# Input projection of a hybrid encoder layer: TensorE's instruction order written out

## The chip, the cores and the metric

The kernel runs on one core of a Trainium2 chip. The core has TensorE (PE, matrix products; its weight loads are shown as PEld), VectorE (DVE), ScalarE (ACT), GpSimd (POOL) and SyncE (SP, which here issues the DMA transfers). The metric is the device time of one execution in microseconds (us); lower is better. Each engine has its own list of instructions, and semaphores make it wait for the others.

## The reference

One layer of a bidirectional encoder, float32, 1024 tokens of width 1024. The part at issue is the mixer: one projection whose columns go to windowed attention and to a gated delta rule.

```python
h = _rms_norm(x, g_mix_pre[l])
proj = h @ w_in[l]
aq, ak, av, dqkv, dgate, dalpha, dbeta = jnp.split(proj, IN_SPLITS, axis=-1)
aq, ak = _rope(aq, positions), _rope(ak, positions)
attn_o = _window_attention(aq, ak, av, attn_sink[l])      # blocks of 128, +-128 tokens
dn_o = _gated_deltanet(dqkv, dgate, dalpha, dbeta, ...)   # conv, l2norm, chunked delta rule, 2 directions
mix = jnp.concatenate([attn_o, dn_o], axis=-1) @ w_out[l]
x = x + _rms_norm(mix, g_mix_post[l])
...
c = _memory_cross_attention(...); f = _swiglu(...)
```

In the delta rule each chunk of tokens needs a triangular solve with the matrix of products k.k, decayed; the kernel forms its inverse from blocks of 32 (the "base inverse") and combines them in two levels (to 64, then to 128).

## The kernel before

The large products are kept close to float32 by splitting: an operand is cast to a high part (`whi`, `hhi`) and the rest is kept as a low part (`wlo`, `hlo`); `split` (lines 102 and 103) does it, the cast on ACT and the subtraction on DVE or POOL. A dense product of the projection is then three matmuls (high by high, low by high, high by low).

The **projection stage** takes 22 tiles of 128 columns of `w_in`. For one tile, `load_w` fetches 512 KB, splits it, and `gemm_b` (line 259) runs 2 halves of 512 tokens x 8 steps of the contraction x 3 matmuls = 48 matmuls of 128x512 into PSUM tile `pg`. Twelve tiles are keys, queries and values of the four delta-rule heads (`D0` to `D3`); four are gates (`G`), five the attention's queries and keys (`A`), one its values (`V`). Behind each tile comes elementwise work: for the delta rule a five-tap convolution (`conv`: ACT copies, four DVE operations at line 284, a silu at 285); for the attention the rotary turn (737 to 743).

A small extra product (`wab`, line 313) gives decay and beta; lines 315 to 388 turn it into `G`, `beta`, `EG` and the sine tables.

The **small products** are float32 matmuls of 128x128 that depend on a tile just finished. `prep` (from line 440) does for each head, in two halves (`part`), the decay products `gm` (459 POOL, 460 PE, `E` on ACT 462), transposes of keys (452) with their squares (ACT 469), k.k to `U` (486, 489), k.q to `pc` and `pm` (493, 496), and transposes of queries and values. `base_inverse` (510) runs for each pair of heads 60 small DVE operations (536, 538) on the stored `U`. `levels` (548) combines blocks: transposes of `Ul` (586), masks `L5` and `L6` (587, 588), products 595 and 601, and stores `Z` to `d_pz`. `window` (624) is one block of the attention: scores `psw` (646) of four heads, a masked maximum on DVE (648), exponentials and scalings on ACT (655, 663), transposes `ptw` (669), a split, weighted sums `pow` (674), and the store of `ao` to `d_mix`. `next_windows` issues two windows, each a generator in two parts, with the second part of the window before in between.

The order in which these are issued is in strings, one letter for a function and digits for its head or tile (lines 36 to 38):

```python
ORDER_1 = "D0 P0 D1 P1 D2 P2 D3 P3 B0 B1".split()
ORDER_2 = "L0 L1 G0 G1 A4 V A0 A1 L2 L3 W W W A2 A3 G2 G3 W".split()
ORDER_3 = ("M " + "s01 W K " * 5 + "s01 K " * 3 + "s01 V V").split()
```

The strings do not settle the order on PE: a scheduler places the instructions of each engine when the program is built, by its own estimates of when inputs are ready, so that dense products of later tiles can stand ahead of small products issued earlier. Stores of `pm` are held in the list `unsaved` and issued by `save` at chosen places.

Then follows the **scan stage** (`ORDER_3`): `s` is a step of the delta rule's recurrence (products `psc`, line 790) on `kv` and `pz` loaded from `d_kv` and `d_pz` (798, 799), `W` the windows that remain, `K` and `V` keys and values of the memory tokens (921, 937). The buffers for these loads lie where the normalised input of the projection was. Output projection, cross-attention and the feed-forward part come after and are not touched.

Of the kernel before, what the change touches and what calls it, by code (L numbers as in the profile page):

```python
# [35 lines left out]
ORDER_1 = "D0 P0 D1 P1 D2 P2 D3 P3 B0 B1".split()  # L36
ORDER_2 = "L0 L1 G0 G1 A4 V A0 A1 L2 L3 W W W A2 A3 G2 G3 W".split()
# [38 lines left out]
def tile_hybrid_block(  # L76
# [176 lines left out]

    def gemm_b(whi, wlo, act, psums, nk=KT):

        for ah, p_ in zip(act, psums):
            for k in range(nk):
                for i, (w, a) in enumerate(((whi, 0), (whi, 1), (wlo, 0))):
                    nc.tensor.matmul(p_, w[:, k, :], ah[a][:, k, :], start=(k == 0 and i == 0),  # L259
                                     stop=(k == nk - 1 and i == 2))  # L260

    def proj(src_cols, eng=None):
        whi, wlo = load_w(src_cols, KT, P, eng)
        pp = [pg.tile([P, 512], F32, tag="pg", name="pg") for _ in range(2)]
        gemm_b(whi, wlo, hT, pp)
        return pp

# [6 lines left out]
    def conv(pp, ci):  # L274
# [3 lines left out]
        acc = tcv.tile([P, S], F32, tag="acc", name="acc", bufs=5)  # L278
        taps = [cols[:, t * 12 + ci:t * 12 + ci + 1] for t in range(5)]
        for hf in range(2):  # L280
            nc.scalar.copy(cp[:, 2 + hf * HALF:2 + (hf + 1) * HALF], pp[hf])
            nc.scalar.activation(acc[:, hf * HALF:(hf + 1) * HALF], pp[hf], AF.Identity, scale=taps[2])  # L282
        for t in (0, 1, 3, 4):
            nc.vector.scalar_tensor_tensor(acc, cp[:, t:t + S], taps[t], acc, ALU.mult, ALU.add)  # L284
        nc.scalar.activation(acc, acc, AF.Silu)
        return acc
# [5 lines left out]
    ws = [load_w(dcols(i, 0), KT, P, after=xload[t]) for i, t in ((1, 1), (0, 3))]  # L292
# [5 lines left out]
    kqv0 = [conv(pps[0], 4), conv(pps[1], 0)]  # L298
# [5 lines left out]
    wabr = t1.tile([P, KT, P], F32R, tag="wabr", name="wabr", bufs=1)  # L304
# [3 lines left out]
    abT = t1.tile([32, S], F32, tag="abT", name="abT", bufs=1)  # L308
    for hf in range(2):
        pp = pg.tile([P, 512], F32, tag="pg", name="pg")  # L310
        for k in range(KT):
            for a in range(2):
                nc.tensor.matmul(pp, wabr[:, k, :], hT[hf][a][:, k, :], start=(k == 0 and a == 0),
                                 stop=(k == KT - 1 and a == 1))
        nc.scalar.copy(abT[:, hf * HALF:(hf + 1) * HALF], pp[0:32, :])
    pt = small()
    for c in range(NT):
        nc.tensor.transpose(pt[:, c * 32:(c + 1) * 32], abT[:, c * P:(c + 1) * P], ident[0:32, 0:32])
    ptv = pt[:, 0:256].rearrange("p (c n) -> p c n", c=NT)
    ab = t1.tile([P, NT, 16], F32, tag="ab", name="ab")  # L320
    nc.scalar.copy(ab, ptv[:, :, 16:32])
    nc.vector.tensor_tensor(ab, ab, ptv[:, :, 0:16], ALU.add)
    dump("ab", ab)

    def s64(n):
        return t1.tile([P, NT, 8], F32, tag=n, name=n)

    xa, za, ua, ea, la = s64("xa"), s64("za"), s64("ua"), s64("ea"), s64("la")
    nc.vector.tensor_tensor(xa, ab[:, :, 0:8], bc(prm[:, 8:16], 1, (P, NT, 8)), ALU.add)
    nc.vector.tensor_scalar(za, xa, -1.0, None, ALU.mult)  # L330
    nc.vector.tensor_tensor(za, za, xa, ALU.min)
    nc.scalar.activation(za, za, AF.Exp)
    nc.vector.tensor_scalar(ua, za, 1.0, None, ALU.add)
    nc.scalar.activation(la, ua, AF.Ln)

    nc.vector.scalar_tensor_tensor(ea, ua, -1.0, za, ALU.add, ALU.subtract)
    nc.vector.reciprocal(ua, ua)
    nc.vector.tensor_tensor(ea, ea, ua, ALU.mult)
    nc.vector.tensor_tensor(la, la, ea, ALU.subtract)
    nc.vector.scalar_tensor_tensor(la, xa, 0.0, la, ALU.max, ALU.add)  # L340
# [3 lines left out]
    nc.vector.tensor_tensor(G.rearrange("p d h c -> p c (d h)"), la, bc(nega, 1, (P, NT, 8)), ALU.mult)  # L344
    nc.scalar.activation(xa, ab[:, :, 8:16], AF.Exp, scale=-1.0)
    nc.vector.tensor_scalar(xa, xa, 1.0, None, ALU.add)
    nc.vector.reciprocal(za, xa)
    nc.vector.tensor_copy(beta.rearrange("p d h c -> p c (d h)"), za)
    dump("G", G)
    dump("beta", beta)  # L350


    pt = small()
    pv = pt[:, 0:192].rearrange("p (s d n) -> p s d n", s=3, d=2)
    for d in range(2):
        gd = G[:, d].rearrange("p h c -> p (h c)")
        for i, m in enumerate((("mUi", "mL", "ones"), ("mLi", "mU", "ones"))[d]):
            nc.tensor.matmul(pv[:, i, d, :], cm[m], gd, start=True, stop=True)
    EG = sm.tile([P, 3, 2, 4, NT], F32, name="EG")
    pv = pt[:, 0:192].rearrange("p (s d h c) -> p s d h c", s=3, d=2, h=4)  # L360
    nc.scalar.activation(EG[:, :, 0], pv[:, :, 0], AF.Exp)
    for c in range(NT):
        nc.scalar.activation(EG[:, :, 1, :, c], pv[:, :, 1, :, NT - 1 - c], AF.Exp)


    MAGIC = 12582912.0
    c1 = 6.28125
    c2 = float(np.float32(np.round((2 * math.pi - c1) * 2.0 ** 21) / 2.0 ** 21))
    c3 = float(np.float32(2 * math.pi - c1 - c2))
    sinT = rt.tile([P, S], F32, name="sinT")  # L370
    cosT = rt.tile([P, S], F32, name="cosT")
    for hf in range(2):
        sl = slice(hf * HALF, (hf + 1) * HALF)
        posi = t1.tile([P, HALF], I32, tag="posi", name="posi", bufs=1)
        nc.sync.dma_start(posi, positions[0, sl].partition_broadcast(P))
        ang = t1.tile([P, HALF], F32, tag="ang", name="ang", bufs=1)
        nc.vector.tensor_copy(ang, posi)
        nc.vector.tensor_scalar(ang, ang, rope_f, None, ALU.mult)
        rn = t1.tile([P, HALF], F32, tag="rn", name="rn", bufs=1)
        nc.vector.tensor_scalar(rn, ang, 1.0 / (2.0 * math.pi), MAGIC, ALU.mult, ALU.add)  # L380
        nc.vector.tensor_scalar(rn, rn, MAGIC, None, ALU.subtract)
        for cc in (c1, c2, c3):
            nc.vector.scalar_tensor_tensor(ang, rn, -cc, ang, ALU.mult, ALU.add)
        nc.vector.tensor_scalar(ang, ang, math.pi, -math.pi, ALU.min, ALU.max)
        nc.scalar.activation(sinT[:, sl], ang, AF.Sin, scale=rope_s)
        nc.scalar.activation(cosT[:, sl], ang, AF.Sin, scale=0.5)
        nc.vector.tensor_tensor(cosT[:, sl], cosT[:, sl], cosT[:, sl], ALU.mult)
        nc.vector.tensor_scalar(cosT[:, sl], cosT[:, sl], -2.0, 1.0, ALU.mult, ALU.add)
    dump("rope", (sinT, cosT))

    pa1.close()
    pa0.close()
# [8 lines left out]
    nEG = sm.tile([P, 2, 4, NT], F32, name="nEG")  # L401
    nc.vector.tensor_scalar(nEG, EG[:, 0], -1.0, None, ALU.mult)
# [13 lines left out]
    unsaved = []  # L416

    def save(after=None):

        while unsaved:  # L420
            with ExitStack() as order_:
                if after:
                    order_.enter_context(tc.issue_after(after.ins))
                nc.sync.dma_start(*unsaved.pop(0))

    def beta_rows(g):
# [8 lines left out]
        nc.tensor.transpose(pt[0:32, 0:P], bp.rearrange("p d h c -> p (d h c)"), ident)  # L435
# [4 lines left out]
    def prep(h, kc, qc, vc):  # L440

        g, hh = h // 2, h % 2
        for src, i in ((kc, 2), (qc, 3)):
            nc.sync.dma_start(d_kv[g][:, :, hh, i].rearrange("c p n -> p c n"), src.rearrange("p (c n) -> p c n", c=NT))
        def part(b):
            c4 = slice(4 * b, 4 * b + 4)

            def turned(src):
                p_ = small()
                for j in range(4):  # L450
                    o = (4 * b + j) * P
                    nc.tensor.transpose(p_[:, j * P:(j + 1) * P], src[:, o:o + P], ident)
                return p_.rearrange("p (c n) -> p c n", c=4)


            pa = small()
            for d, (mi, ml) in enumerate((("mUi", mL_s), ("mLi", mU_s))):
                gm = t2.tile([P, 4, P], F32, tag="gm", name="gm")
                nc.gpsimd.tensor_tensor(gm, bc(G[:, d, h, c4], 2, (P, 4, P)), bc(cm[mi], 1, (P, 4, P)), ALU.mult)
                nc.tensor.matmul(pa, ml, gm.rearrange("p c n -> p (c n)"), start=(d == 0), stop=(d == 1))  # L460
            E = t2.tile([P, 4, P], F32, tag="E", name="E")
            nc.scalar.activation(E, pa.rearrange("p (c n) -> p c n", c=4), AF.Exp)

            def squares(pk, rev):
                ss = t2.tile([P, 4], F32, tag="ss4", name="ss4", bufs=4)
                for j in range(4):
                    jk = t2.tile([P, P], F32, tag="jk", name="jk")
                    o = 3 - j if rev else j
                    nc.scalar.activation(jk, pk[:, j, :], AF.Square, accum_out=ss[:, o:o + 1])
                return ss  # L470

# [7 lines left out]
            if hh and b:  # L479
                beta_rows(g)  # L480
# [24 lines left out]
            if h < 3:  # L505
                save()
# [3 lines left out]
    def base_inverse(g):  # L510
# [7 lines left out]
        if g:  # L518
            save(load)
# [1005 lines left out]
```

## Time and profile before

| | |
|---|---|
| three runs | 1581.2, 1585.76, 1586.17 us (median 1585.76) |
| profiled execution | 1581.95 us, its span 1580.1 us, mean clock of PE 0.985 |
| first dense product of the projection | at 24.0 us |
| last dense product of the projection | at 393.95 us |
| first product of the scan | at 405.64 us |
| first product of the output projection (`pmg`) | about 596 us |
| PE busy | 1503.9 us, 95% |

A row of the timeline gives the start in us, the length in us, the engine, the line of the kernel, the operation, output tile <- input tiles, shapes and how many records the row joins; in brackets the idle time before it and what ended it. Matmuls are pipelined, so the time that one takes is read from start to start of the next. A float32 product counts as two records, a transpose as one. Rows of the groups give the count, then the total busy time in us and the mean in ns, then the idle time of the engine just before and its releasers. PE's clock is the share that the chip granted, 1.00 being full.

### The profile page before, as it was taken

The page shows a single profiled execution, that of the slowest core. Times are in us where ns is not written, and L with a number is a line of the kernel's source. Part 1 is how long each engine was busy: PE and PEld are TensorE (multiplying, and loading weights), DVE is VectorE, ACT ScalarE, POOL GpSimd, SP SyncE. Part 2 cuts the span into 40 slices and gives each one's busy share as a digit, 9 for nine tenths or more (in the row PEclk, how much of TensorE's full clock was granted, in tenths as well). Part 3 has the DMA queues.
Part 4 walks back from the last instruction along what each step waited for, and adds up shares of the span by engine and source line. Part 5 has one row for each costly group of instructions (what it writes and reads, how often), then busy time and mean ns, then how long its engine had stood idle before and what let it go on. Part 6 is the DMA issues. An engine that isn't in the chain of part 4 may idle for free.

```text
span 1580.1 us, 21010 instructions
## 1 busy us (share of the span) xinstructions
PE 1503.9 (95%) x7451; PEld 1256.4 (80%) x7451; DVE 1047.9 (66%) x1609; ACT 748.8 (47%) x1504; POOL 462.1 (29%) x432
## 2 busy tenths in 40 slices
PE   6999898999899989999999999999999999999998
PEld 5777777778799867788888777788888888888786
DVE  6855977965688865444346448777768654586665
ACT  6564452246866764564335566332232332444532
POOL 2364433232234500253301140433434433100021
PEclk9999999999999999999999999999999999999999
DMA  6244337473998585454222264443335333853354
GB/s 208 67 129 120 107 107 180 134 187 111 318 293 276 164 271 184 157 187 147 74 73 94 67 206 139 125 150 121 127 110 164 100 101 106 294 202 112 107 171 162
DMA packets 260485, 242.95 MB, mean 154 GB/s; under 512 B 33672, under 2 KB 199453, under 8 KB 260381
## 3 DMA queue, kind: packets, MB, share of 16 engines
q1 hardware_dynamic: 260381, 241.62, 48.6%
q8 instruction: 58, 0.95, 0.2%
q14 instruction: 46, 0.38, 0.1%
HBM read 172.07 MB, written 66.88 MB: 151 GB/s over the span
## 4 chain that ended last, share of the span: by engine, by line
PE 74%; DVE 11%; DMA 6%; ACT 4%; issue 2%; SPq 1%; POOL 1%; DVEq 0%; POOLq 0%; ACTq 0%
PE pmg L1021 10%; PE pD L1196 7%; PE pE L1196 7%; PE pg L259 7%; PE pA L1196 6%; PE pcq L259 6%; PE pdX L1386 5%; PE pdA L1386 4%; PE pB L1196 4%; PE psc L790 3%; DVE acc L284 3%; PE pdD L1386 2%; PE pcs L1102 1%; PE pco L1128 1%; PE pck L921 1%
## 5 line engine op out<-in xcount | busy, mean ns | idle before, releaser
L102 ACT CAST whi<-wraw 128x1024 fp32r<-128x1024 f32 x108 | 113.1, 1049 | 149.7 <-DMA wraw<-in_w_gate_up_dram 30.9
L103 POOL TENSOR_TENSOR wlo<-wraw,whi 128x1024 fp32r<-128x1024 f32 x48 | 117.9, 2456 | 191.1 <-ACT whi L102 168.6
L259 PE MATMUL pg<-hhi,whi 128*128 128x512 f32 x352 | 141.0, 401 | 0.0
L259 PE MATMUL pg<-hhi,wlo 128*128 128x512 f32 x352 | 140.8, 400 | 0.0
L259 PE MATMUL pg<-hlo,whi 128*128 128x512 f32 x352 | 140.3, 399 | 0.0
L103 DVE TENSOR_TENSOR wlo<-wraw,whi 128x1024 fp32r<-128x1024 f32 x60 | 74.4, 1243 | 76.8 <-ACT whi L102 72.6
L1021 PE MATMUL pmg<-whi,b 128*128 128x512 f32 x384 | 118.4, 395 | 2.7 <-ACT whi L102 2.2
L1196 PE MATMUL pA<-s,whi 128*128 128x512 f32 x352 | 109.6, 392 | 1.4 <-ACT m L1213 1.4
L284 DVE SCALAR_TENSOR_TENSOR acc<-cp,cols,acc 128x1024 f32<-128x1024 f32 x48 | 77.2, 1610 | 19.2 <-ACT acc L282 14.0
L1021 PEld LDWEIGHTS pmg<-whi,b 128*128 128x128 f32 x384 | 71.2, 188 | 17.9 <-ACT whi L102 2.7
L259 PEld LDWEIGHTS pg<-hhi,whi 128*128 128x128 f32 x352 | 67.2, 191 | 14.4 <-issue 0.7
L259 PEld LDWEIGHTS pg<-hlo,whi 128*128 128x128 f32 x352 | 67.1, 191 | 14.2 <-issue 1.0
L259 PEld LDWEIGHTS pg<-hhi,wlo 128*128 128x128 f32 x352 | 67.4, 191 | 13.6 <-issue 0.5
L1386 PE MATMUL pdX<-dhl,whi 128*128 128x512 f32 x264 | 76.1, 390 | 1.5 <-DVE zv L1441 0.8
L1196 PEld LDWEIGHTS pA<-s,whi 128*128 128x128 f32 x352 | 65.3, 188 | 15.2 <-ACT m L1213 2.0
L1273 POOL TENSOR_TENSOR act<-act,up 128x512 f32<-128x512 f32 x33 | 50.1, 1519 | 88.0 <-DVE up L1272 53.2
L1021 PE MATMUL pmg<-wlo,b 128*128 128x512 f32 x192 | 71.4, 392 | 0.0
L1196 PE MATMUL pA<-s,wlo 128*128 128x512 f32 x176 | 68.7, 391 | 1.1 <-DVE wlo L103 1.1
L102 ACT CAST whi<-araw 128x1024 fp32r<-128x1024 f32 (+1 forms) x36 | 35.4, 982 | 71.5 <-PE pdX L1386 27.6
L1416 POOL TENSOR_SCALAR frs<-sq 128x1 f32<-128x1 f32 x8 | 11.9, 1497 | 195.5 <-ACT jk L1405 194.6
L1245 POOL TENSOR_TENSOR sr<-wraw 128x512 f32<-128x512 f32 x22 | 29.9, 1359 | 128.5 <-DMA wraw<-in_w_gate_up_dram 128.4
L103 DVE TENSOR_TENSOR wlo<-araw,whi 128x1024 fp32r<-128x1024 f32 (+1 forms) x36 | 40.8, 1133 | 39.5 <-ACT whi L102 39.4
(408 smaller groups left out, 4158.9 us busy)
## 6 DMA issues: line engine op xcount, KB each, us to landing
wraw<-in_w_gate_up_dram SPq DMA_DIRECT2D x52, 512.0 KB, 3.9
kv<-d_kv SPq DMA_DIRECT2D x32, 512.0 KB, 7.3
wraw<-in_w_in_dram SPq DMA_DIRECT2D x22, 512.0 KB, 4.7
b<-in_w_down_dram SPq DMA_DIRECT2D x20, 512.0 KB, 6.8
araw<-d_as SPq DMA_DIRECT2D x20, 512.0 KB, 3.7
pz<-d_pz SPq DMA_DIRECT2D x32, 256.0 KB, 7.1
wraw<-in_w_ckv_dram SPq DMA_DIRECT2D x16, 512.0 KB, 7.6
wraw<-in_w_out_dram SPq DMA_DIRECT2D x16, 512.0 KB, 4.1
```

Of the source, the lines that this page charges most:

```text
L102: nc.scalar.copy(hi, src)
L103: (eng or nc.vector).tensor_tensor(lo, src, f32(hi), ALU.subtract)
L259: nc.tensor.matmul(p_, w[:, k, :], ah[a][:, k, :], start=(k == 0 and i == 0), stop=(k == nk - 1 and i == 2))
L284: nc.vector.scalar_tensor_tensor(acc, cp[:, t:t + S], taps[t], acc, ALU.mult, ALU.add)
L790: nc.tensor.matmul(out[:, d, h, :], lt[:, d, h, :], rt[:, d, h, :], start=True, stop=True)
L921: nc.tensor.matmul(pp, w[:, k, :], mT[a][:, k, :], start=(k == 0 and i == 0), stop=(k == KT - 1 and i == 2))
L1021: nc.tensor.matmul(pp[t], act[a][:, k, tt], w_[:, kk, :], start=(k == 0 and i == 0), stop=(k == KT - 1 and i == 2))
L1102: nc.tensor.matmul(pp[:, t2_, :], q[a][:, ct, tt], kr_[b_][:, ct, :], start=(j == 0 and i == 0), stop=(j == 1 and i == 2))
L1196: nc.tensor.matmul(out_, w[a][:, k, :], xx[b_][:, k, :], start=(start and k == 0 and i == 0), stop=(k == HK - 1 and i == 2), skip_group_ch ...
L1245: nc.gpsimd.tensor_tensor(s[0], b_[:, 0:HK], b_[:, HK:], ALU.add)
L1273: nc.gpsimd.tensor_tensor(o_, o_, up, ALU.mult)
L1386: nc.tensor.matmul(banks[t], a[:, k - k0, tt], w, start=(first and k == 0 and i == 0), stop=(k == NB - 1 and i == 2), skip_group_check=not ...
```

## The change

The order of PE's instructions in the projection stage is written out and kept.

- A list `TILES` names the 22 weight tiles in order; the first two are now the keys of heads 0 and 1 (before, key and query of head 0). They are still left to the scheduler.
- After them every matmul and transpose of the stage goes through `mm` and `turn`, which tell the builder to keep PE's instructions in program order.
- The dense products are issued step by step (a step or position is three matmuls, 0 to 31 being the first two tiles; the last is 352). `PLAN` gives the position at which each piece of `prep` is issued: K transposes and squares of keys, E decay, U k.k, C k.q, Q and S transposes of queries and values, B beta rows. `LEVELS` starts the pieces of `levels` at 232, 2.4 positions apart; `WINDOWS` starts those of the first windows at 300, 0.72 apart; `WINDOWS_AHEAD` = 4 counts the pairs of windows in the stage. The decay work runs at positions 35, 51 and 58.
- A tile's results are taken off `half` by `half`; there are 6 buffers of `acc` instead of 5, 4 of `E` instead of 2.
- The key and value rows of `d_kv` are stored separately (`kt`, `vt`) instead of together (`kv`): eight more stores with runs of half the length. The list `unsaved` is gone: `pm` is stored at once. `Ul` is loaded earlier, for both halves of a head.
- In a window, the weighted sum of a block comes one block after its transposes.

The counts of products and of elementwise operations stay. ACT's table loads go from 27 to 23.

```diff
-ORDER_1 = "D0 P0 D1 P1 D2 P2 D3 P3 B0 B1".split()
-ORDER_2 = "L0 L1 G0 G1 A4 V A0 A1 L2 L3 W W W A2 A3 G2 G3 W".split()
+TILES = "k0 k1 q0 v0 q1 v1 k2 k3 q2 v2 q3 v3 G0 G1 A4 V A0 A1 A2 A3 G2 G3".split()
+PLAN = {
+    "K0": (36, 39), "K1": (44, 47), "E0": (50, 52), "E1": (54, 56), "U0": (59, 61), "U1": (66, 68), "B0": (71,),
+    "C0": (74, 76), "Q0": (79, 82), "S0": (87, 90), "C1": (99, 101), "Q1": (104, 107), "S1": (115, 118),
+    "E2": (109, 111), "E3": (113, 121), "K2": (131, 133), "U2": (136, 138), "K3": (147, 149), "U3": (152, 154),
+    "B1": (157,), "C2": (163, 165), "Q2": (168, 171), "S2": (179, 182), "C3": (195, 197), "Q3": (200, 203),
+    "S3": (211, 214),
+}
+LEVELS = (232, 2.4)
+WINDOWS = (300, 0.72)
+WINDOWS_AHEAD = 4
...
+    def mm(*a, **k):
+        t = nc.tensor.matmul(*a, **k)
+        if pinned[0]:
+            tc.keep_in_program_order(t)
...
-    ws = [load_w(dcols(i, 0), KT, P, after=xload[t]) for i, t in ((1, 1), (0, 3))]
+    ws = [load_w(dcols(1, h), KT, P, after=xload[t]) for h, t in ((0, 1), (1, 3))]
...
-            kv = t2.tile([P, 4, 2, P], F32, tag="kv", name="kv")
...
-                        unsaved.append((d_pz[g][d][c4, :, hh, 0].rearrange("c p n -> p c n"), pm))
...
+        elif what == "K":
+            pk = turned(kqv["k", h], cs)
+            kt = t2.tile([P, 4, P], F32, tag="kt", name="kt")
+            nc.scalar.copy(kt, pk)
+            nc.sync.dma_start(d_kv[g][c4, :, hh, 0].rearrange("c p n -> p c n"), kt)
+            ss = squares(pk, False)
...
+        def weighted(j, halves):
+            for i, pe_ in enumerate(halves):
+                mm(po.rearrange("p h t -> p (h t)"), vhl[:, k0 + j, g].rearrange("p r e -> p (r e)"), pe_,
+                   start=(j == 0 and i == 0), stop=(j == nb - 1 and i == 1))
...
+    jobs, now, count = [], [32], iter(range(10000))
+    def at(pos, fn):
+        jobs.append((pos, next(count), fn))
...
+    for pos in (35, 51, 58):
+        at(pos, lambda: next(dec))
+    for what, steps in PLAN.items():
+        k, h = what[0], int(what[1])
+        for b, pos in enumerate(steps):
+            at(pos, (lambda h=h: beta_rows(h)) if k == "B" else (lambda k=k, h=h, b=b: prep(k, h, b)))
...
+    at(215, to_levels)
+    lp = level_pieces()
+    for i in range(41):
+        at(LEVELS[0] + (i - 3 if i else -6) * LEVELS[1], lambda: next(lp))
...
+    for i in range(20 * WINDOWS_AHEAD):
+        at(WINDOWS[0] + i * WINDOWS[1], window_piece)
...
+    for tok in TILES[2:]:
+        src, eng, half = weight_tile(tok[0], int(tok[1:] or 0))
+        whi, wlo = load_w(src, KT, P, eng)
+        for hf in range(2):
+            p_ = pg.tile([P, 512], F32, tag="pg", name="pg")
+            for k in range(KT):
+                for i, (w, a) in enumerate(((whi, 0), (whi, 1), (wlo, 0))):
+                    mm(p_, w[:, k, :], hT[hf][a][:, k, :], start=(k == 0 and i == 0), stop=(k == KT - 1 and i == 2))
+                if k == KT - 1:
+                    half(hf, p_)
+                now[0] += 1
+                due(now[0])
+    due(1e9)
+    pinned[0] = False
```

`to_levels` issues both base inverses and opens the pools of the levels and windows; `due` runs the jobs whose position has come; `weight_tile` gives a tile's columns and what is done with each of its halves.

More of the change, by code (lines that the diff above doesn't have):

```diff
@@ L260, in gemm_b @@
                                      stop=(k == nk - 1 and i == 2))
[L262 to L266, printed above, removed]
     pa1.close()
@@ L312, in tile_hybrid_block @@
             for a in range(2):
[L313 to L314 removed]
+                mm(pp, wabr[:, k, :], hT[hf][a][:, k, :], start=(k == 0 and a == 0), stop=(k == KT - 1 and a == 1))
         nc.scalar.copy(abT[:, hf * HALF:(hf + 1) * HALF], pp[0:32, :])
[L316 to L318 removed]
@@ L366, in tile_hybrid_block @@
[L366 to L369, printed above, removed]
+    EG = sm.tile([P, 3, 2, 4, NT], F32, name="EG")
+    nEG = sm.tile([P, 2, 4, NT], F32, name="nEG")
     sinT = rt.tile([P, S], F32, name="sinT")
     cosT = rt.tile([P, S], F32, name="cosT")
[L372 to L388, printed above, removed]
@@ L620, in part @@
                 nc.sync.dma_start(d_pz[g][d][c4, :, hh, 1].rearrange("c p n -> p c n"), Z[d])
-        together([part(b) for b in range(2)])
+        parts = [part(b) for b in range(2)]
+        for _ in range(5):
+            for g_ in parts:
+                next(g_, None)
+                yield
     def window(n, g):
@@ L769, in tile_hybrid_block, with issue @@
     pgs.close()
+    def issue(order, table):
+        for o in order:
+            table[o[0]](*(int(c) for c in o[1:]))
     p2 = ExitStack()
```

426 lines of the change are left out of this document (251 added, 175 removed).

## The prediction

> **What bounds the kernel now.** I read the engine shares first, then 50-us slices of the first 450 us, where the changed code runs, then what TensorE (PE) waited for there, then single products in the timeline.
>
> ```profile
> PE 1503.9 (95%) x7451; PEld 1256.4 (80%) x7451; DVE 1047.9 (66%) x1609; ACT 748.8 (47%) x1504; POOL 462.1 (29%) x432
> ```
>
> PE is the bound on average. The slices (start:end, then us and busy time with instruction counts of PE, its weight loads, DVE, ACT and POOL, then granted clock, DMA share, GB/s) show where it is not:
>
> ```profile
> 150.00:200.00 50.00, 44.87 (x212) 36.20 (x211) 45.23 (x64) 20.98 (x54) 19.72 (x23) 0.97 0.38 113
> 200.00:250.00 50.00, 46.26 (x220) 36.95 (x219) 31.49 (x40) 24.32 (x59) 15.75 (x15) 0.97 0.51 141
> 250.00:300.00 50.00, 43.66 (x220) 36.40 (x218) 48.12 (x93) 13.39 (x31) 17.21 (x12) 0.93 0.59 145
> 300.00:350.00 50.00, 44.45 (x229) 38.40 (x230) 35.86 (x70) 19.45 (x50) 17.14 (x15) 0.90 0.74 184
> 350.00:400.00 50.00, 47.92 (x280) 40.94 (x278) 30.19 (x76) 33.92 (x80) 13.63 (x13) 1.00 0.43 125
> 400.00:450.00 50.00, 43.38 (x289) 39.31 (x290) 35.44 (x95) 36.61 (x85) 11.21 (x12) 0.90 1.05 336
> ```
>
> The waits of PE in 0 to 400 us (total us, times, longest), the largest rows after the start-up:
>
> ```profile
> PE ps L595 <- DVE L L588: 6.2, 2, 3.9
> PE ps L460 <- POOL gm L459: 4.9, 2, 3.7
> PE ps L486 <- DVE U L489: 3.6, 1, 3.6
> PE ps L586 <- DVE Z L618: 3.1, 1, 3.1
> PE ps L586 <- DMA Ul<-d_u: 2.0, 2, 1.8
> ```
>
> These make 19.8 us; smaller rows add 5. The slow clock costs 50 x (0.03 + 0.03 + 0.07 + 0.10) = 11.5 us. So the projection stage loses about **36 us**, and most of it follows a late small product. The timeline shows one such wait (start, length, then the product):
>
> ```profile
> 299.22 0.39 PE L259 MATMUL pg<-hlo,whi 128*128 128x512 f32 x1
> 301.88 3.27 PE L595 MATMUL ps<-m,L 128*128 128x32 f32 x16 [2.28 <-DVE L L588]
> ...
> 305.54 0.63 PE L259 MATMUL pg<-hhi,whi 128*128 128x512 f32 x1
> 305.96 0.63 PE L259 MATMUL pg<-hlo,whi 128*128 128x512 f32 x1
> ```
>
> After an idle of 2.28 us the dense products start 0.42 us apart.
>
> ```profile
> 80.12 1.95 PE L486 MATMUL ps<-acc 128*128 128x128 f32 x16
> 81.82 0.47 PE L259 MATMUL pg<-hhi,whi 128*128 128x512 f32 x1
> 82.14 0.39 PE L259 MATMUL pg<-hlo,whi 128*128 128x512 f32 x1
> 82.36 0.39 PE L259 MATMUL pg<-hhi,wlo 128*128 128x512 f32 x1
> ...
> 390.74 0.33 PE L646 MATMUL psw<-khi,qs 128*128 128x384 f32 x1
> 390.92 0.33 PE L646 MATMUL psw<-klo,qs 128*128 128x384 f32 x1
> ...
> 410.40 0.60 PE L669 MATMUL ptw<-ident,sc 128*128 128x128 f32 x4
> 410.83 1.30 PE L790 MATMUL psc<-kv,pz 128*128 128x128 f32 x8
> ```
>
> Start to start a dense product takes 0.23 us when warm, but 0.32 just behind fp32 products (81.82 to 82.14); 16 records of fp32 products take 1.70, four transposes 0.43, a score 0.18. A position of the new plan is three dense products, 0.68 us.
>
> **The change part by part.**
>
> *PE's own work in the stage: +24.* Counted in the two instruction orders up to the last dense product, window scores go from 30 to 64, window transposes from 20 to 80, weighted sums from 10 to 38: 34 x 0.18 + 15 groups x 0.43 + 28 x 0.23 = 19 us, moved here from the scan stage. The dense run is also cut more often: some 60 more returns from fp32 products at 0.09 make 5.
>
> *The 36 us of present losses* belong to this order and go: **-36**. What the new order loses stands in their place. The old one lets dense products pass a small product whose input is late; the new one holds everything behind it.
>
> *The start, positions 35 to 56.* Both key tiles come first, so ACT gets the squares of four key halves together with the decay's table loads:
>
> ```profile
> L102 ACT CAST whi<-wraw 128x1024 fp32r<-128x1024 f32 x20 | 21.0, 1052 | 19.4 <-PE pg L259 16.0 <-POOL pm L496 2.8 <-issue 0.5
> L469 ACT ACTIVATE jk<-ps 128x128 f32<-128x128 f32 x64 | 17.0, 295 | 9.0 <-PE ps L452 9.0
> L469 ACT ACTIVATION_READ_ACCUMULATOR jk<-ps 128x1 f32 x64 | 14.4, 226 | 0.0
> L285 ACT ACT_TABLE_LOAD x7 | 9.0, 1283 | 27.3 <-DVE acc L284 27.3
> L655 ACT ACTIVATE sc<-sc,nm 128x384 f32<-128x384 f32 (+1 forms) x16 | 9.2, 579 | 2.9 <-DVE nm L653 2.8
> L655 ACT ACTIVATION_READ_ACCUMULATOR sc<-sc,nm 128x1 f32 x15 | 2.8, 188 | 0.0
> L663 ACT ACTIVATE sc<-sc,es 128x384 f32<-128x384 f32 (+1 forms) x12 | 6.0, 570 | 0.8 <-DVE es L661 0.7
> L102 ACT CAST ph<-ptw 128x512 fp32r<-128x512 f32 x6 | 3.4, 573 | 0.0
> ...
> L103 POOL TENSOR_TENSOR wlo<-wraw,whi 128x1024 fp32r<-128x1024 f32 x10 | 25.3, 2532 | 18.6 <-DVE ang L378 13.5 <-ACT whi L102 4.9
> L459 POOL TENSOR_TENSOR gm<-G,C 128x512 f32<-128x512 f32 x16 | 21.3, 1338 | 11.2 <-DVE G L344 7.0 <-PE ps L460 4.1
> ```
>
> (Rows of the groups: busy us, mean ns, idle before.) Before the next whi, ACT has 14 squares x 0.52 + 3 loads x 1.28 + some six copies of about 0.57 + a silu near a cast's 1.05 + the cast: 17 us. PE needs 12 for positions 35 to 48 (13 x 0.68 and the transposes). POOL's wlo (2.53) waits for that whi, and the gm (1.34) of position 52 is queued behind wlo: 3.9 us, against about 5 of PE. So gm is 4 us late, E and all products behind it too. With a wait of up to 3 for abT behind silu and sines at position 35, and a slow clock after, I take **+10** (5 to 14).
>
> *The first level product, position 232.* Its operand L is in DVE's queue behind nearly the whole second base inverse and three convolutions.
>
> ```profile
> L284 DVE SCALAR_TENSOR_TENSOR acc<-cp,cols,acc x48: 1273/1284/3414, 46.1 to 220.7; 128x1024 f32<-128x1024 f32 x48
> ...
> L536 DVE TENSOR_TENSOR tmpb<-A 128x30 f32<-128x30 f32 (+14 forms) x60 | 32.0, 533 | 1.3
> L538 DVE TENSOR_TENSOR A<-A,tmpb 128x30 f32<-128x30 f32 (+14 forms) x60 | 24.3, 406 | 1.6
> ```
>
> (The first row has minimum, median and maximum ns.) One base inverse is 30 x (0.533 + 0.406) = 28. With 12 convolution taps x 1.28 = 15 and about 20 of weight splits, block copies and masked copies (some 25 operations of 0.5 to 1.3) between positions 163 and 232, DVE has 63; PE has 69 x 0.68 and 9 of small products, 56. L is 7 late; with the clock **+8** (0 if DVE has a lead of 7 at 163; 14 at the longer tap times). The levels behind it go piece by piece at 1.6 us, ACT and DVE between: **+3** (0 to 8).
>
> *The windows, positions 303 to 352.* ACT has 31 exponentials x 0.77, 28 scalings x 0.57, 19 splits x 0.57, 7 loads x 1.28 and about 18 of the rest (query and weight casts 7, outputs and gates 6, level copies 5): 79 us. PE has 49 positions (33), 7 windows of products (28) and the last level with restarts (10): 71. The first weights also take four exponentials and four scalings, over 5 us, after their scores, with PE given 3 positions. ACT is the bound: **+12** (6 to 16). All other waits, DMA queues among them: **+3** (0 to 6). The eight extra stores, the earlier pm stores and the smaller runs of the split store go to arrays that are read only after 400 us: nothing; a queue delay would be in the last term. The four table loads saved are in the count of ACT.
>
> *The scan stage.* 19 us of PE work have left it. But they covered something:
>
> ```profile
> 394.18 1.00 PE L601 MATMUL ps<-bs,D 128*128 128x64 f32 x8
> ...
> 405.64 0.61 PE L790 MATMUL psc<-kv,pz 128*128 128x128 f32 x4
> ...
> DMA to landing us min/median/max: 4.2/7.3/9.3
> ```
>
> From the last dense product to the first scan product pass 11 us, mostly window products. After, that gap waits for the last attention store's turn on SP and the kv load (third row): about 8, uncovered. So 19 minus 8 of lost cover plus 3 of shorter gap, 14; the slice from 400 has a DMA share of 1.05, so some is lost there too: **-12** (-20 to -4).
>
> Sum: 24 - 36 + 10 + 8 + 3 + 12 + 3 - 12 = +12. The profiled execution took 1581.95 (span 1580.1): **1594**. The median shown, 1585.76, is 3.8 above that execution, so 1594 is 0.5% above the median.
>
> The Trainium skill ("TensorE: Matmul & The Clock Gate", Part 1: The HAM clock gate) puts the fall to half rate after an idle window of about 3.4 us. The trace does not quite agree: 2.28 us sufficed. By the page, waits of 2 to 3 us would cost no clock; as an estimate the sum would then be some 5 lower, 1589.
>
> **The rivals.**
> - *Faster: the steps between are long enough.* For it: in the old order the dense filler reached PE anyway, and idle is only 25 of 370 us; if the new waits come to 15 instead of 36 and 18 of the moved work is saved, 24 - 36 + 15 - 18 = -15: **1567**. It decides at positions 303 to 352: only where ACT keeps under PE's 71 us. Against it: the three sums above, each over PE's time.
> - *No change:* the new waits come to 25 and 13 is saved: **1582**; also what comes out if the written order were not kept in the built program, which the instruction order excludes.
> - *Much slower:* the window stage runs as a chain (scores, exponentials, scalings, transposes), each of seven windows 3 us late instead of 1.7, and slow clock after each; new waits of 50, 5 saved: 24 - 36 + 50 - 5 = +33: **1615**. For it: the slow products at 305; against: scores stand one window ahead.
>
> **How the numbers follow.** Forecast (1586 to 1606, its own range) 0.40, faster rival 0.32, no change 0.17, much slower 0.11. About 0.3% (4.7 us) is what a measurement can tell from no change. Faster 0.32; within 0.16; slower 0.52. The range takes in the faster rival with room below, and the upper bounds of the waits: 1560 to 1612.
>
> **What would show it.** In the changed profile: 64 scores and some 80 transposes of windows before the last dense product; PE waits on POOL gm near 80 us, on DVE L near position 232, on ACT ph or the softmax tiles near the end; ACT nearly full in the last 80 us of the stage; last dense product near 415 us instead of 394; from there to the first product of the output projection some 12 us less than before. I am wrong if the listed PE waits of the stage stay under 15 us, or if the stage ends before 400.

## The result and the profile after

| | before | after |
|---|---|---|
| median | 1584.39 us (1581.2 to 1586.17) | 1644.47 us (1636.27 to 1646.6) |
| ratio, 95% interval | | 1.0372 (1.0331 to 1.0413) |
| profiled span, mean clock of PE | 1580.1 us, 0.985 | 1641.0 us, 0.972 |
| last dense product of the projection | 393.95 us | 462.26 us |
| first product of the scan | 405.64 us | 470.05 us |
| first product of the output projection | 595.91 us | 655.52 us |

The changed kernel is 3.7% slower, 60 us where +12 was forecast. The direction was right; the size was not, and the time lies outside the range. The busy shares of the profiled execution after:

```profile
PE 1527.4 (93%) x7451; PEld 1265.0 (77%) x7451; DVE 1046.4 (64%) x1609; ACT 747.4 (46%) x1500; POOL 466.9 (28%) x432
```

The counts are the old ones (ACT has the four table loads less). PE's busy time is 23.5 us longer at the same count, which is slow clock. The timeline of PE places the loss (start, length, product, and in brackets the idle before it):

```profile
462.26 0.40 PE L268 MATMUL pg<-hhi,wlo 128*128 128x512 f32 x1
...
470.05 1.20 PE L924 MATMUL psc<-kv,pz 128*128 128x128 f32 x4 [4.73 <-DMA pz<-d_pz]
...
655.52 0.62 PE L1155 MATMUL pmg<-whi,s 128*128 128x512 f32 x2
...
750.32 0.62 PE L282 MATMUL pcq<-b,whi 128*128 128x512 f32 x2
```

The same view of the kernel before:

```profile
595.91 1.22 PE L1021 MATMUL pmg<-whi,s 128*128 128x512 f32 x2 [2.84 <-ACT vv L941]
...
690.89 0.61 PE L259 MATMUL pcq<-b,whi 128*128 128x512 f32 x2
```

The projection stage ends 68.3 us later; the scan stage, from the last dense product to the first `pmg`, gives back 8.7; at the first product of the cross-attention (`pcq`) the difference is 59.4, and at the end of the span 60.9. So nearly the whole result lies ahead of 655 us. The slices after (as in the prediction, and then the stage, its end from 350 us, and the scan stage):

```profile
150.00:200.00 50.00, 50.00 (x249) 40.67 (x248) 41.00 (x49) 26.94 (x64) 27.25 (x24) 0.99 0.54 143
200.00:250.00 50.00, 46.71 (x218) 38.65 (x217) 46.09 (x69) 16.93 (x51) 16.52 (x15) 0.93 0.46 132
250.00:300.00 50.00, 41.40 (x212) 34.75 (x211) 34.28 (x64) 15.13 (x35) 15.30 (x12) 0.90 0.67 158
300.00:350.00 50.00, 44.52 (x247) 37.50 (x247) 28.52 (x51) 16.39 (x41) 14.88 (x11) 0.97 0.50 136
350.00:400.00 50.00, 41.56 (x216) 32.78 (x215) 32.22 (x79) 31.87 (x82) 14.05 (x14) 0.93 0.38 107
400.00:450.00 50.00, 39.34 (x157) 29.87 (x156) 18.85 (x50) 34.56 (x71) 7.24 (x11) 0.86 0.21 61
...
24.00:462.30 438.30, 386.42 (x1866) 309.68 (x1865) 295.78 (x497) 212.17 (x510) 150.29 (x143) 0.94 0.42 113
350.00:462.30 112.30, 90.55 (x412) 69.98 (x411) 55.76 (x143) 75.15 (x171) 22.77 (x27) 0.89 0.28 81
462.30:655.50 193.20, 165.69 (x1140) 150.82 (x1139) 128.99 (x306) 112.53 (x275) 54.91 (x64) 0.92 0.83 267
```

From 400 to 450 us no engine is near full: PE has 39 of 50 us, at a clock of 0.86, and fewer products (157) than in any slice above. That is a stretch in which engines wait for each other. The waits of PE from 24 to 462.3 us (total, times, longest):

```profile
PE pow L268 <- ACT ph L113: 14.5, 8, 2.9
PE ps L268 <- POOL gm L495: 10.8, 4, 7.3
PE ps L268 <- DVE mov L631: 7.7, 5, 2.2
PE ps L268 <- DVE tmpb L551: 6.1, 1, 6.1
PE ps L273 <- ACT acc L305: 3.3, 1, 3.3
PE pow L268 <- DVE pl L114: 2.5, 10, 0.4
PE ptw L273 <- ACT sc L688: 2.3, 1, 2.3
PE psw L268 <- DVE m L671: 2.2, 3, 1.3
PE ps L273 <- ACT abT L339: 1.7, 2, 1.4
```

They sum to 51 us (438.3 less the busy 386.4 gives 52), and the clock of 0.94 costs 438.3 x 0.06 = 26: 78 us lost in the stage, where the old order lost 36. The wait named first is at the end of the stage, where a window's weighted sum wants the cast `ph` of its transposed weights:

```profile
418.24 1.04 PE L273 MATMUL ptw<-ident,sc 128*128 128x128 f32 x8
...
419.57 0.40 PE L268 MATMUL pg<-hhi,wlo 128*128 128x512 f32 x1
422.84 0.50 PE L268 MATMUL pow<-ph,vhl 128*128 128x512 f32 x1 [2.87 <-ACT ph L113]
423.57 0.78 PE L268 MATMUL pow<-pl,vhl 128*128 128x512 f32 x1 [0.22 <-DVE pl L114]
424.14 0.63 PE L268 MATMUL pg<-hhi,whi 128*128 128x512 f32 x1
424.57 0.63 PE L268 MATMUL pg<-hlo,whi 128*128 128x512 f32 x1
```

And ACT in the same microseconds:

```profile
417.74 0.62 ACT L660 CAST qs<-qr 128x512 fp32r<-128x512 f32 x1 [2.20 <-PE psw L268]
418.38 1.28 ACT L680 ACT_TABLE_LOAD   x1
419.68 0.61 ACT L680 ACTIVATE sc<-sc,nm 128x384 f32<-128x384 f32 x1
...
421.49 0.60 ACT L680 ACTIVATE sc<-sc,nm 128x384 f32<-128x384 f32 x1
421.99 0.19 ACT L680 ACTIVATION_READ_ACCUMULATOR sc<-sc,nm 128x1 f32 x1
422.20 1.07 ACT L113 CAST ph<-ptw 128x512 fp32r<-128x512 f32 x2
```

The transposes end near 419.3. The cast of their result stands on ACT behind a table load and four exponentials of the *next* window, and starts at 422.20. Meanwhile PE's next instruction in the kept order is the sum that needs this cast, so the dense products behind it, whose operands lie ready, cannot start. Just before, ACT had itself been idle for 2.20 us until PE had done scores. After the wait dense products start 0.43 us apart instead of 0.23.

### The profile page after: what moved, and what is told of

The parts are those of the page before. It is cut to its first block, busy times and chain, and to the rows that moved or that the text cites. A ratio compares the mean times of both kernels' runs of the same rounds, so it can differ in the third digit from the quotient of the medians.

```text
span 1641.0 us, 21051 instructions
## 1 busy us (share of the span) xinstructions
PE 1527.4 (93%) x7451; PEld 1265.0 (77%) x7451; DVE 1046.4 (64%) x1609; ACT 747.4 (46%) x1500; POOL 466.9 (28%) x432
## 5 line engine op out<-in xcount | busy, mean ns | idle before, releaser
L268 PE MATMUL pg<-hhi,wlo 128*128 128x512 f32 x320 | 130.1, 407 | 0.0
L268 PE MATMUL pg<-hlo,whi 128*128 128x512 f32 x320 | 129.5, 405 | 0.0
L268 PEld LDWEIGHTS pg<-hhi,wlo 128*128 128x128 f32 x320 | 62.8, 196 | 14.9
L268 PEld LDWEIGHTS pg<-hlo,whi 128*128 128x128 f32 x320 | 63.6, 199 | 11.4 <-issue 2.2
L268 PEld LDWEIGHTS pg<-hhi,whi 128*128 128x128 f32 x320 | 63.5, 198 | 10.6 <-issue 2.2
```

What stands on the lines that cost most here:

```text
L268: t = nc.tensor.matmul(*a, **k)
```

## The experiments

Each edit is to the changed kernel unless it says otherwise. Ratios are to the kernel before, run beside it. Its own median was between 1583.4 and 1588.0 us from group to group, so edits are better compared by their ratios. The changed kernel's ratio, 1.0372, has an interval of 0.4%, or 6.5 us, either way.

| edit | median us | ratio (95%) | last dense product, us |
|---|---|---|---|
| a: nothing kept | 1580.52 | 0.9966 (0.9953 to 0.9978) | 394.6 |
| b: kept only up to position 299 | 1587.29 | 1.0013 (0.9996 to 1.0030) | 404.9 |
| i: kept only from position 300 | 1642.47 | 1.0364 (1.0331 to 1.0397) | 457.2 |
| f: kernel before, keys first | 1588.24 | 1.0000 (0.9982 to 1.0017) | 396.7 |
| g: no windows in the stage | 1608.13 | 1.0153 (1.0121 to 1.0185) | 389.0 |
| g: half of the windows | 1599.78 | 1.0103 (1.0074 to 1.0133) | 420.9 |
| c: softmax in portions | 1633.55 | 1.0303 (1.0280 to 1.0327) | 460.1 |
| j: scalings on DVE | 1637.54 | 1.0325 (1.0306 to 1.0343) | 453.4 |
| j and c together | 1640.30 | 1.0327 (1.0309 to 1.0345) | 454.7 |
| l: nothing kept, scalings on DVE | 1584.40 | 0.9987 (0.9974 to 1.0000) | 396.6 |
| m: kernel before, scalings on DVE | 1601.69 | 1.0090 (1.0075 to 1.0105) | 399.3 |
| n: windows without ACT's softmax | 1616.21 | 1.0175 (1.0132 to 1.0218) | 437.6 |
| o: dense products free from 300 | 1594.55 | 1.0053 (1.0032 to 1.0074) | 398.3 |
| d: decay of two heads earlier | 1644.79 | 1.0383 (1.0343 to 1.0424) | 466.5 |

### a: nothing kept

The issue order, tiles, buffers and stores of the change stay; only PE's order is again the scheduler's.

```diff
-    pinned = [True]
+    pinned = [False]
```

> The changed kernel with nothing kept in program order: tiles, plan, levels and windows are issued at the same positions, but the scheduler places PE's instructions. Theory (the kept order costs by itself: PE idles 52 us in waits between 24 and 462 us and loses 26 us of clock behind them, because dense products cannot pass a late small product): most of the 78 us goes, last dense product at 400 to 425 us instead of 462, time 1590 to 1610. Rival (ACT and DVE simply have too much work in the stage since the windows were moved in): the dense end stays beyond 445 us, time 1630 or more. Rival (the new order of tiles is what costs): 1630 or more as well.

1580.52 us, less than expected, and the last dense product at 394.6 is earlier than expected too. The whole loss comes from keeping the order: left to the scheduler, the rest of the change costs nothing. This version is the fastest of all, 0.34% under the kernel before. Which other part of the change gives that gain was not separated; the new first tiles alone do not (f).

### b: kept only up to position 299

```diff
+                if now[0] == 300:
+                    pinned[0] = False
```

> The changed kernel with the order kept only to position 299; the last levels, the windows and the dense products from 300 on are left to the scheduler. Theory (the windows' part of the kept order costs most: 21 us of waits on ACT ph, DVE m and DVE pl after 350 us and 12 us of slow clock): 20 to 33 us faster than the changed kernel, 1612 to 1625. Rival (ACT is the bound there with 79 us of work): less than 8 us faster, 1637 or more.

Much more came back than expected: 57 of the 60 us. The order up to 299, with all small products of `prep` and most of `levels`, costs 1587.29 - 1580.52 = 7 us against the free one. The end of the stage in this kernel:

```profile
350.00:404.90 54.90, 54.56 (x295) 46.84 (x294) 31.19 (x73) 34.31 (x78) 16.78 (x18) 1.00 0.47 136
```

At 350 us nearly the same dense work is left as in the changed kernel (165 recorded products here, 158 there). Here it is done in 55 us, PE full and the clock at 1.00; with the order kept it takes 112, with more products of the windows among it (64 scores instead of 28).

### i: kept only from position 300

The complement: `pinned` starts as False and becomes True at 300.

> The counterpart of b_winfree: the order is left to the scheduler up to position 299 and kept from 300 on, windows included (64 scores, 80 transposes and 38 weighted sums again stand before the last dense product). Theory (the kept window part costs some 50 us, the kept order before it some 7 to 10, and the two add): 1625 to 1640. Rival (the two interact: dense products that the scheduler leaves for the end fill the windows' waits, or the losses before 300 only matter together with those behind): under 1610.

1642.47 us: all of the loss, from 53 steps of 353, and 2.5 us above the expected range. Over the free kernel, 7 us (b) and 62 (here) make 69, where the whole order costs 64: within the intervals the two add. Its wait on `ph` from 350 us is that of the changed kernel, a little larger:

```profile
PE pow L268 <- ACT ph L113: 15.7, 10, 2.9
```

### f: the kernel before, keys of heads 0 and 1 first

```diff
-    ws = [load_w(dcols(i, 0), KT, P, after=xload[t]) for i, t in ((1, 1), (0, 3))]
+    ws = [load_w(dcols(1, h), KT, P, after=xload[t]) for h, t in ((0, 1), (1, 3))]
...
```

> The kernel before with one part of the change alone: the first two tiles are the keys of heads 0 and 1. Theory: the order of tiles costs little, within 6 us of the kernel before (1579 to 1591). Rival (keys ahead crowds ACT at the start and costs much of the 60 us): 1600 or more.

The order of the first tiles makes no difference that can be measured under the scheduler.

### g: none, or half, of the windows in the stage

```diff
-WINDOWS_AHEAD = 4
-ORDER_3 = ("M " + ...
+WINDOWS_AHEAD = 0
+ORDER_3 = ("M W W W W " + ...
```

> Order kept throughout, as in the changed kernel, but no window is issued in the projection stage; the four pairs are issued behind the memory norm at the start of the scan stage, where nothing is kept. Theory (what costs is that the kept order holds windows ahead of the last dense products; in the scan stage they fill idle time): last dense product at 390 to 405 us, scan stage 200 to 212 us instead of 193, time 1583 to 1600. Rival (a kept order costs wherever it is, and the last 52 positions would wait for something else): last dense product beyond 430 us, 1615 or more.

> Order kept, two pairs of windows in the stage instead of four and at twice the distance (1.44 positions), the other two pairs at the start of the scan stage. Theory (work moved plus waits, both halved or less): waits on ph under 5 us, 1595 to 1615. Rival (only the amount of moved work matters, not the waits): 1625 to 1635, half way to g_none at the most with waits on ph of 7 us or more.

(For half: `WINDOWS_AHEAD = 2`, a spacing of 1.44, and "M W W ".) The stage does end sooner with fewer windows: 462.3, 420.9, 389.0 for four, two and no pairs, so each pair costs about 18 us of the stage. With half of them the time is in its range, though the waits on `ph` came to 5.7 us and not under 5. The kernel without them came out above its range, at 1608: the last of its windows (scores up to 634.6 us) run beside the output projection, which starts at 594.3, and its first `pcq` is at 717.6, 27 us later than before. Where windows go is a trade; half is the better of these, and neither reaches the free kernel.

### c, j: shorten what stands ahead of the cast

c issues the exponentials and scalings of a window in three portions between the blocks of the window before; j moves the scalings from ACT to DVE; a third run has both.

```diff
-            if hh < 3:
-                yield False
+            yield hh == 3
...
+            soft = True
+            for _ in last or ():
+                yield False
+                soft = soft and not next(w)
...
-            nc.scalar.mul(pr[hh][:, 0:w], pr[hh][:, 0:w], es[:, hh:hh + 1])
+            nc.vector.tensor_scalar(pr[hh][:, 0:w], pr[hh][:, 0:w], es[:, hh:hh + 1], None, ALU.mult)
```

> The changed kernel, order kept, but the exponentials and scalings of a window are issued in three portions between the blocks of the window before, so that on ACT at most two exponentials (1.5 us) stand ahead of a ph cast, instead of four (3.1 us). Theory (PE's six waits of up to 2.9 us for ph come from ACT's queue order, and each costs slow clock behind it): waits on ph fall from 14.5 to under 7 us, 8 to 18 us faster than the changed kernel, 1626 to 1636. Rival (ACT's amount of work): waits on ph stay within 3 us of 14.5, time within 5 us of 1644.

> The changed kernel with the four scalings of each window (L688, 2.1 us per window on ACT) moved to DVE, which is busy 19 of 50 us there; order kept. Theory (in the kept window part PE and ACT wait for each other in turn, so what counts is how long a window's chain on ACT lasts, not that ACT is full: it is busy 35 of 50 us): each of seven windows gets about 2 us shorter, waits on ph fall, 8 to 20 us faster than the changed kernel, 1624 to 1636. Rival (PE's own moved work, some 30 us of products and restarts, is what the part costs): within 5 us of 1644.

> Both edits of c_soft and j_dve: exponentials in portions and scalings on DVE, order kept. Theory (the chain): more than either alone, waits on ph under 5 us, 1612 to 1628. It still stays above 1600, since the 30 us of products moved in front of the last dense ones remain. Rival (one and the same wait is removed by both): as the better of the two, 1625 to 1634.

The wait on `ph` from 350 us, in c:

```profile
PE pow L268 <- ACT ph L113: 10.4, 9, 2.0
```

14.5 became 10.4 in c, 12.5 in j and 7.9 in both. So what stands ahead of the cast on ACT does set a part of this wait. But the kernel gained only 11, 7 and 4 us by the medians (11, 7 and 7 by the ratios), and the last two gains are hardly clear of the noise. In j the wait on the low part `pl`, which DVE makes, grew from 2.5 to 4.3; with both edits, PE's time from the last dense product to the first `pcq` grew from 288.0 to 293.5 us. Of the expectations, c's time came true but not its wait (under 7); j's time is 1.5 us above its range; both together missed.

### l, m: the scalings on DVE without the kept order

The edit of j, in the kernel with nothing kept and in the kernel before.

> a_free (nothing kept in order) with the scalings on DVE. Theory (where the scheduler may pass a late product, ACT's chain in the windows is covered, so its length matters little): within 5 us of a_free, 1576 to 1586. Rival (the chain is on the path of the scan stage too): 1570 or less.

> The kernel before with the scalings on DVE, as control of l_free_dve. Theory: within 5 us of the kernel before, 1580 to 1590. Rival as for l_free_dve: 10 us faster or more.

The kernel before loses 0.9% by it, which was not expected; the free one some 4 us, hardly outside its interval. In the kernel before with this edit, the waits on `pl` between the last dense product and the first `pcq` went from 2.7 us (6 times) to 6.0 (6 times), and the busy time of DVE there from 201.7 to 226.9 of some 300 us. The free kernel shows much the same (waits on `pl` from 1.1 to 5.5 us, DVE from 201.6 to 216.9), so these waits do not tell the two apart: why the edit costs the kernel before more than the free one stays open. It gained time, if at all, only where the order is kept.

### n: windows without ACT's softmax

For the windows of the projection stage, the exponentials with their negated maxima and sums, and the scalings, are left out; the mask is added to the first columns. Small operations on DVE and POOL that belong to them go too. All matrix products, transposes, casts and sums stay in their places.

```diff
+        bare = pinned[0]
+        if bare:
+            band = C[:, 0:w]
...
+        if not bare:
+            nm = tw.tile([P, 4], F32, tag="nm", name="nm")
...
+            for hh in range(4):
+                nc.scalar.mul(pr[hh][:, 0:w], pr[hh][:, 0:w], es[:, hh:hh + 1])
```

> The changed kernel, order kept and every product in its place; for the windows issued in the projection stage the band mask, the exponentials with their maxima and sums, and the scalings are left out, so that ACT has only the ph casts and small copies of them. The windows of the scan stage are whole. Theory (of the 57 us that the window part is longer than in b_winfree, 24 are the moved products and restarts and 33 are waits on the windows' chain and slow clock): the waits on ph, m and sc and most of the slow clock after 350 us go; last dense product at 428 to 440 us instead of 462, time 1608 to 1622. Rival (the amount of moved products): last dense product beyond 450 us, 1632 or more.

As the theory expected. Its slice from 350 us to its last dense product, and its waits there:

```profile
350.00:437.60 87.60, 82.50 (x430) 67.32 (x429) 52.05 (x122) 30.83 (x59) 23.18 (x21) 0.96 0.38 109
```

```profile
PE pow L268 <- ACT ph L113: 1.9, 2, 1.5
PE pow L268 <- DVE pl L114: 1.8, 3, 0.9
```

With the chain through ACT gone, 16 of the 21.5 us of waits and 9 of the 12 us of clock go (87.6 x 0.04 = 3.5 remain), and the stage ends 24.7 us sooner. What is left, 437.6 against 404.9 in b, is mostly the moved products themselves (from 350 us PE is busy for 82.50 us here and for 54.56 in b). This edit takes ACT's work away together with its place in the queue, so it does not say how much is due to the place alone; c, which changed the place, took 4 of the 14.5 us.

### o: dense products free from position 300

The small products and the windows keep their order among themselves; only the dense products may pass them.

```diff
-                    mm(p_, w[:, k, :], hT[hf][a][:, k, :], start=(k == 0 and i == 0), stop=(k == KT - 1 and i == 2))
+                    (mm if now[0] < 300 else nc.tensor.matmul)(
+                        p_, w[:, k, :], hT[hf][a][:, k, :], start=(k == 0 and i == 0), stop=(k == KT - 1 and i == 2))
```

> The changed kernel with the small products and windows kept in program order throughout, and only the dense products from position 300 on left to the scheduler (in the built order 24 scores instead of 64 stand before the last dense product). Theory (it is the dense products held behind windows that cost, not the order of the small ones): as b_winfree, last dense product at 395 to 410 us, 1580 to 1595. Rival (the kept order of the windows' own products costs): 1610 or more.

```profile
350.00:398.30 48.30, 48.30 (x256) 41.39 (x254) 26.30 (x63) 30.45 (x68) 13.02 (x13) 1.00 0.39 114
```

PE is full, the clock 1.00, with no wait from 350 us. Now only 24 scores, 20 transposes and 8 sums of windows stand before the last dense product, instead of 64, 80 and 38. 50 of the 60 us come back. This tells the cause from its rival, that keeping windows and small products in order is in itself dear: what costs most is the *dense* product that stands in the queue behind a late small one. By the ratios 6 us over b and 14 over the free kernel remain; the order up to 299 is 7 of these 14, and the rest was not separated.

### d: decay of heads 2 and 3 earlier

The longest wait of all (7.34 us, ended by `gm`) was not foreseen. These rows of the changed kernel's timeline, PE, DVE, ACT and POOL in turn, show where it comes from:

```profile
138.77 0.40 PE L268 MATMUL pg<-hhi,wlo 128*128 128x512 f32 x1
146.50 2.08 PE L268 MATMUL ps<-gm,mL_s 128*128 128x512 f32 x2 [7.34 <-POOL gm L495]
...
140.33 2.28 DVE L304 SCALAR_TENSOR_TENSOR acc<-cp,cols,acc 128x1024 f32<-128x1024 f32 x1
...
142.64 1.06 ACT L305 ACTIVATE acc<-acc 128x1024 f32<-128x1024 f32 x1 [8.69 <-DVE acc L304]
143.61 0.26 ACT L472 ACTIVATE jk<-ps 128x128 f32<-128x128 f32 x1
...
144.81 0.35 POOL L520 TENSOR_SCALAR epsq<-ss 128x4 f32<-128x4 f32 x1 [1.97 <-ACT jk L472]
145.24 2.37 POOL L495 TENSOR_TENSOR gm<-G,C 128x512 f32<-128x512 f32 x2
```

`gm` stands on POOL behind an `epsq`, which needs squares from ACT; these stand behind a silu, which waits for the last convolution tap on DVE; and the taps there share DVE with the base inverse. The edit moves E2 from 109 and 111 to 94 and 96, and E3 from 113 and 121 to 111 and 121.

> The changed kernel with one step moved: the decay products of head 2 at positions 94 and 96 instead of 109 and 111 (those of head 3 at 111 and 121), so that their gm does not stand on POOL behind the pm products and the epsq of head 1. Theory (each wait in the kept order, with the slow clock behind it, adds to the end one for one): the wait of 7.3 us at 139 us and 3 us of slow clock go, 7 to 11 us faster than the changed kernel, 1633 to 1637. Rival (a wait removed here is waited for later, since DVE and ACT set the pace): within 3 us of 1644.

The long wait on `gm` is gone (7.3 at the most in the changed kernel, 1.4 here), and the median is the same to 0.3 us, with intervals of some 6.5 us. PE and ACT a little later in that run:

```profile
168.48 1.12 PE L273 MATMUL ps<-ident,acc 128*128 128x128 f32 x4 [8.40 <-ACT acc L305]
...
166.07 1.28 ACT L305 ACT_TABLE_LOAD   x1 [12.16 <-DVE acc L304]
167.37 1.06 ACT L305 ACTIVATE acc<-acc 128x1024 f32<-128x1024 f32 x1
```

The wait has moved to the transposes of the next convolution's result, whose silu waited 12.16 us for DVE. PE's idle time up to 350 us did not fall (32.6 us here, 30.1 in the changed kernel). The rival fits: DVE sets the pace here, and `gm` only showed it.

## Why the prediction was right in direction and wrong in size

- **PE's own work, +24: right.** The forecast counts of window products stand in the profile (64 scores, 80 transposes before the last dense product). After n takes ACT's chain away, the 437.6 - 404.9 = 33 us that remain over b are these 24 and 8.5 of waits and clock (5.0 and 3.5).
- **The old losses go, -36:** what stands in their place is larger by itself. Up to 350 us the changed kernel loses 30.4 us of waits (10.8 + 7.7 + 6.1 + 3.3 + 1.7 and 0.8 of two small ones) and 26 - 12 = 14 of clock: 44, about 8 more than the old order in its whole stage. b less a measures 7, which agrees.
- **The start, +10: too high.** `gm` and `abT` (the input of the decay's transposes) cost 3.4 + 1.7 = 5 us there, and the clock did not fall (no wait there over 1.4).
- **The first level product, +8: right.** 6.1 us on DVE, and slow products behind it (the slice from 250 us, clock 0.90).
- **The levels behind it, +3, and all other waits, +3: too low.** The pieces of the levels waited 7.7 us on `mov`, a tile that copies on ACT and DVE fill between two products. The 7.34 us before `gm` and the 3.3 before the transposes of a convolution's result were not seen: the prediction followed POOL and ACT at the start only, and DVE only up to position 232's operand, not to the silu in ACT's queue in front of other heads' squares. With their clock the four forecast terms up to 350 us make 44, not 24.
- **The windows, +12 because "ACT is the bound": this step failed.** ACT's work was sized well (79 us, though its terms add up to 78; 75.15 busy from 350 us on). But ACT was not nearly full as forecast: it was busy for 34.56 of 50 us from 400. The step took the longer of two sums, as if each engine could work ahead. In a kept order they work in turn: PE stands at a sum that needs a cast, the cast behind the next window's exponentials, those behind scores that PE has not reached. From 350 us that is 21.5 us of waits and 112.3 x 0.11 = 12.4 of clock: 34 instead of 12. With the moved work, 24 + 34 = 58, against the difference of 57.4 (112.3 and 54.9) between this kernel and b. n and o show it from both sides: take ACT's chain away, or let the dense products pass, and most of it goes.
- **The scan stage, -12: -8.7.** The row of the scan stage before:

```profile
394.00:595.90 201.90, 181.69 (x1270) 165.32 (x1268) 154.31 (x381) 146.07 (x366) 65.59 (x78) 0.96 0.84 263
```

16 us of PE's busy time left it (181.69 to 165.69; not 19, since the clock fell from 0.96 to 0.92), but PE's idle time rose from 20.2 to 27.5 us. The gap from the last dense product to the first scan product is 7.8 us, 4.73 of them waiting for a load of `pz`. The forecast had about 8, but named the load of `kv`.

The sum with the measured sizes, 24 - 36 + 44 + 34 - 9 = +57, stands against 59.4 at `pcq`. The direction had a chance of no more than 0.52, and the terms up to 350 us were 20 too low and the windows 22, so that it was right says little. Of the rivals, "much slower: the window stage runs as a chain" named the mechanism. It had 0.11, because scores stand one window ahead; that did not help, since the exponentials that they allow are what delays the cast. Its price was too low as well: 50 of new waits and clock, where 44 + 34 = 78 were measured.

The Trainium skill ("TensorE: Matmul & The Clock Gate", Part 1: The HAM clock gate) puts the fall to half rate after an idle window of about 3.4 us. The wait of 2.87 us above does not agree: slow products follow it. They also follow the waits of 2.89 and 2.86 us that end at 430.84 and 443.28. Near 2 us it goes either way: one of 1.98 us, ended at 312.93, has slow products 1.8 us behind it, and one of 2.00, ended at 341.82, has none; what decides there stays open. A plan that trusted the 3.4 us would have taken these waits as cheap.

## What to carry to other kernels

A kept order turns every late small product into a stop for all the work behind it; keep the order among the small products if that is wanted, but leave the large ready ones free to pass. Here the fastest was to keep nothing. When an order is written by hand across two engines that feed each other, do not compare the sums of their work: follow one piece through both queues, and look at what stands ahead of it in each. A wait removed by moving its last producer earlier comes back a little later if another engine sets the pace (here DVE, three queues behind the name in the wait).

## What was not expected of the hardware

Some small DVE operations took as long as a POOL operation that ran beside them. From the timeline of the changed kernel:

```profile
127.40 2.40 DVE L551 TENSOR_TENSOR tmpb<-A 128x168 f32<-128x168 f32 x1
...
130.21 0.35 DVE L551 TENSOR_TENSOR tmpb<-A 128x184 f32<-128x184 f32 x1
...
127.16 2.46 POOL L114 TENSOR_TENSOR wlo<-wraw,whi 128x1024 fp32r<-128x1024 f32 x1 [1.92 <-ACT whi L113]
```

The operation on 168 columns, a product of two parts of `A` in SBUF, took 2.40 us and ended with POOL's (129.80 and 129.62); the larger one behind it, with POOL idle, took 0.35. It happens again at 152.56 (2.46 us, beside a POOL operation of 2.63). The Trainium skill ("GPSIMD Engine Reference", 1. Specifications) says that POOL and DVE share their SBUF interfaces and get in each other's way when a DVE instruction has two SBUF inputs. The rows agree, and show the size: a whole POOL operation, for one small DVE operation. Two of the convolution taps ahead of the 7.34 us wait were longer in the same way, 1.70 and 2.28 us beside POOL's `pm` products, though one of 1.27 also ran beside them. No run here separates it from other causes.
